# The first forty microseconds of an encoder block: norm weights by transposition, a new load order, and the engines' order written by hand

## The chip, the cores and the metric

The kernel runs on one core of a Trainium2 chip. The metric is the device time of one execution in microseconds (us); a run's figure is the time of the core from launch to end, and a profiled execution also has a span, from its first to its last recorded instruction. Lower is better.

The engines are called by the short names of the profile: PE (TensorE, matmuls; PEld is its weight load), DVE (VectorE), ACT (ScalarE), POOL (GpSimd) and SP (SyncE, which here issues all the DMA transfers).

## The reference

One block of an encoder on a sequence of 1024 tokens with 16 learned meta tokens in front, width 1024, in float32:

```
h = concat(meta, x)                                   # 1040 x 1024
n = rms_norm(h, norm_mix)
proj = n @ w_in            # qa ka va (512 each) | qb 512 | kb 128 | vb 128 | gates ga, gb (1024 each)
y_a = differential attention of 4 heads over all tokens (two softmaxes, difference, rms_norm)
y_b = windowed attention: 8 query heads, 2 key/value heads, window 128, sinks, meta keys
h = h + (sigmoid(ga) * (y_a @ w_ba) + sigmoid(gb) * (y_b @ w_bb)) @ w_o
h = h + (silu(rms_norm(h, norm_ffn) @ w_gate) * (rms_norm(h, norm_ffn) @ w_up)) @ w_down
out = rms_norm(h, norm_final)[16:]
```

`rms_norm(x, g)` is `x * rsqrt(mean(x*x) + 1e-6) * g`.

## The kernel before

**Precision.** Every float32 operand of a matmul is split into a high part (`fp32r`, written by ACT with Copy) and a low part (the difference, written by DVE or POOL); helper `split`, L116 to L118. A product is three matmuls: high x high, high x low, low x high.

**The beginning.** The normed tokens are needed transposed, in `hT_hi` and `hT_lo` (width on the 128 partitions, tokens along the row). Tokens come in tiles of 128: tiles 0 to 7, and `NT`, the 16 meta tokens. For each tile there are three steps:

- `load_x(t)`: SP issues the load of 512 KB into a buffer with the tag `btr`, of which there are four. Tile 4 takes the buffer of tile 0, and so on.
- `norm_x(t)` calls `normed` (L131 to L141): a Square with a running sum on ACT (L134), two small operations on POOL for the reciprocal root (`rstd_of`, L122 and L123), and on DVE one pass that multiplies by it and by the norm weights `gmix` (L140). `gmix` is a tile of 128 x 1024: the 1024 weights, the same in each partition. The kernel before loads it with one DMA that reads the row 128 times.
- `turn_x(t)` calls `transposed` (L143 to L151): twice four transpositions on PE against an identity (L148), the high parts by ACT (L150), the low parts by DVE (L151).

**The first projections.** Three blocks of 128 columns of `w_in` are projected while the tiles come in: kb (`C_KB`), and two blocks of qb, here q0 (`C_QB`) and q1 (`C_QB + P`). `prep` loads a block's weights (1024 rows of 512 bytes, tag `w`, two buffers) and splits them (POOL writes the low part of kb's, DVE that of the q blocks). `project_steps` is a generator: for each chunk of tokens (256 each, kb's last 272) it gives eight steps of three matmuls (L214), and after the eighth an eviction: high part by ACT into one of three stage buffers (tag `qk`), low part by DVE, and then copies by DMA from the stage to `kb` (eight for each chunk, L282, and for the last eight more, L285) or to `qb` (four, L305). `advance(n)` takes the next n steps of the generators in the list `early`, each entry giving one chunk; `ensure(n)` prepares weights ahead. Chunk i needs the tiles 2i and 2i+1. The projection of vb follows, and then the attention in blocks (`attend_b`), whose scores are evicted at L333 with the distance table `tbx` and the sinks `nsink`; these are computed from `iota` (L469 to L477) and small loads (L484 to L499). On POOL, sums of halves of `hT` (`token_sums`, L525 to L539) are wanted for the gates; they need all eight tiles.

**Who sets the order.** The kernel is written in Tile. Where nothing else is said, a planner that simulates the program with its own costs orders each engine's instructions, so that an instruction that stands late in the code may run early. Within `tc.manual_schedule()` the engines (or those named) keep the order of the code. Before, such sections exist only for later parts (POOL from the second half of the windowed attention, PE from the differential attention on, all engines in the last product); the beginning is the planner's.

**Filler matmuls.** Products of zeros into a PSUM bank `idle` that nobody reads keep PE running ahead of the first real work: 15 before the first transpositions and 7 after (L413, L426).

**Activation tables.** ACT loads a table of functions before it uses a function that the current one lacks. There are three such loads: at the start, ahead of the first Sigmoid of the gates (L1010), and ahead of the first Silu (L1304).

Of the kernel before, what the change touches and what calls it, by code (L numbers as in the profile page):

```python
# [19 lines left out]
P = 128  # L20
S = 1024
D = 1024
NM = 16
L = S + NM
DC = D // P
# [48 lines left out]
def encoder_block(ctx: ExitStack, tc: tile.TileContext, x, meta, norm_mix, w_in, lq1, lk1, lq2, lk2,  # L74
# [7 lines left out]
    def f32(ap):  # L82
        return ap.bitcast(F32)
# [76 lines left out]
    def pp_bank(name):  # L160
        return bank(psum1, "pp", name, 3 if psum1 is not psum2 else PP2)
# [45 lines left out]
    def project_steps(col, chunks, name, evac):  # L207
        wh, wl = prepped.pop(col)
        terms = [(wh, hT_hi), (wh, hT_lo), (wl, hT_hi)]
        for at, n in chunks:  # L210
            ps = pp_bank(f"pp_{name}_{at}")
            for c in range(DC):
                for i, (a, b) in enumerate(terms):
                    nc.tensor.matmul(ps[:, :n], a[:, c, :], b[:, c, at:at + n],  # L214
                                     start=(c == 0 and i == 0), stop=(c == DC - 1 and i == 2))
                if c == DC - 1:
                    evac(ps[:, :n], at, n)
                yield
# [51 lines left out]
    vb = [(bpool if g else vtpool).tile([P, 9, P], F32R, tag=("q1", "vb")[g], name=f"vb{g}", bufs=1) for g in range(BG)]  # L270
    mds = [bpool.tile([P, 4, P], F32, name=f"bmd{i}") for i in range(2)]
    for i in range(2):
        nc.gpsimd.memset(f32(vb[i])[:, 8, :], 0.0)
        nc.gpsimd.memset(mds[i], 0.0)

    def kb_consume(st, at, n):
# [103 lines left out]
    def load_x(t):  # L380
        xts[t] = bpool.tile([P, D], F32, tag="btr", name=f"x_{t}", bufs=4)
        if t < NT:
            nc.sync.dma_start(xts[t], x[t * P:(t + 1) * P, :])
        else:
            nc.sync.dma_start(xts[t][:NM], meta)
# [24 lines left out]
    nc.vector.memset(zeros, 0.0)  # L410
    idle = bank(psum1, "by", "idle", 1)
    for _ in range(15):
        nc.tensor.matmul(idle, zeros[:, 0:P], zeros, start=True, stop=True)  # L413
    load_x(0)
    nc.sync.dma_start(gmix, norm_mix.broadcast_to([P, D]))
    load_x(1)
    ensure(1)
    norm_x(0)
    load_x(2)
    norm_x(1)  # L420
    xn0 = xns[0]
    turn_x(0)
    zeros = bpool.tile([P, 512], BF16, tag="by1", name="zeros", bufs=2)
    nc.vector.tensor_scalar(zeros, xn0[:, 0:512], 0.0, None, ALU.mult)
    for _ in range(7):
        nc.tensor.matmul(idle, zeros[:, 0:P], zeros, start=True, stop=True)  # L426
    ensure(2)
    load_x(3)
    norm_x(2)
    turn_x(1)  # L430
    p_kb = project_steps(C_KB, KB_CHUNKS, "kb", evac_split(None, kb_consume))
    p_q0 = qb_steps(0, qb, 0)
    p_q1 = qb_steps(0, qb, 1)
    prepped[C_QB + P] = prep(C_QB + P, "qbx", lowpool, nc.vector)
    early += [(p_kb, DC), (p_q0, DC), (p_q1, DC)]
    advance(E_STEPS)
    norm_x(3)
    turn_x(2)
    advance(E_STEPS)
    load_x(4)  # L440
    norm_x(4)
    turn_x(3)
    early += [(p_kb, DC), (p_q0, DC), (p_q1, DC)]
    advance(E_STEPS)
    load_x(5)
    norm_x(5)
    turn_x(4)
    advance(E_STEPS)
    load_x(6)
    load_x(NT)  # L450
    norm_x(6)
    turn_x(5)
    early += [(p_kb, DC), (p_q0, DC), (p_q1, DC)]
    advance(E_STEPS)
    load_x(7)
    norm_x(7)
    norm_x(NT)
    turn_x(6)
    advance(E_STEPS)
# [24 lines left out]
    nc.sync.dma_start(gsub, subln.rearrange("o p -> p o"), allow_slow_non_contiguous=True)  # L484
    nc.vector.tensor_scalar(gsub, gsub, 1.0 - LAMBDA_INIT, None, ALU.mult)
    sinkb = acon.tile([P, BH], F32, name="sinkb")
    nc.sync.dma_start(sinkb, sink.broadcast_to([P, BH]))
# [3 lines left out]
    lam_in = bpool.tile([P, 4, HD], F32, tag="by1", name="lam_in", bufs=2)  # L491
# [3 lines left out]
    nc.vector.tensor_tensor(lam_p, lam_in[:, 0::2, :], lam_in[:, 1::2, :], ALU.mult)  # L495
# [1016 lines left out]
```

## Time and profile before

| | us |
|---|---|
| median of 3 runs | 1451.38 |
| lowest and highest | 1447.25, 1451.52 |
| the profiled execution's own time | 1446.1 |
| its span | 1444.3 |

Busy time in the profile counts what an engine executes; for PE the ends of matmuls are modelled, since they are pipelined. The timeline lists an instruction's start, its duration, engine, line, operation and tiles (written <- read), and in brackets how long the engine was idle before it and who ended that. "SPq" rows are DMA issues in SP's queue. The chain of waits follows the work that ended last back through what released each step. Views of waits give total, number and longest.

### The profile page before, as it was taken

How to read it: one execution, taken by the hardware profiler on the slowest of the kernel's cores; microseconds unless marked ns; L12 is line 12 of the kernel's file. 1: busy time of each engine (PE TensorE's matmuls, PEld its weight loads, DVE VectorE, ACT ScalarE, POOL GpSimd, SP SyncE). 2: the span in 40 equal slices, each digit the busy share in tenths (PEclk: the TensorE clock that was granted, in tenths of full speed). 3: DMA queues.
4: the chain of work that ended last, by engine and by line, in shares of the span. 5: the costliest groups of instructions: out<-in, count | busy, mean ns of one | idle time of the engine just before them, and what ended most of it. 6: DMA issues, size and time to landing. Idle time of an engine off the chain costs nothing.

```text
span 1444.3 us, 21160 instructions
## 1 busy us (share of the span) xinstructions
PE 1422.8 (99%) x7279; PEld 1221.2 (85%) x7279; DVE 899.2 (62%) x1624; ACT 679.6 (47%) x1290; POOL 641.3 (44%) x605
## 2 busy tenths in 40 slices
PE   8999999999999999999999999999999999999997
PEld 6988989988898999888888878888888888888886
DVE  7478536637697989624614966554555553787567
ACT  6366535545665656544413643333333333444454
POOL 5599127743333333334522665544544452000444
PEclk9999999999999999999999999999999999999999
DMA  8467658986557473576612534333332332964443
GB/s 244 90 209 237 193 162 265 288 281 213 190 169 257 147 227 125 190 256 209 216 34 88 152 104 161 109 102 110 102 102 96 110 102 102 331 208 140 124 129 139
DMA packets 188891, 242.41 MB, mean 168 GB/s; under 512 B 18208, under 2 KB 115936, under 8 KB 188784
## 3 DMA queue, kind: packets, MB, share of 16 engines
q1 hardware_dynamic: 188784, 241.07, 52.6%
q8 instruction: 57, 0.93, 0.3%
q14 instruction: 50, 0.41, 0.1%
HBM read 157.45 MB, written 77.00 MB: 162 GB/s over the span
## 4 chain that ended last, share of the span: by engine, by line
PE 81%; POOL 6%; DVE 5%; issue 4%; DMA 2%; ACT 1%; POOLq 0%; SPq 0%; DVEq 0%; ACTq 0%
PE pg L1293 28%; PE pd L1387 9%; PE pg L737 7%; PE po L1070 6%; PE ppa L780 6%; PE aps L796 3%; PE pp_qb L214 3%; POOL oa L118 3%; PE apy L835 3%; PE pp_ka L214 2%; PE pp_va L214 2%; PE apt L822 2%; PE pp_qa L214 2%; PE bpt L356 1%; PE bpy L362 1%
## 5 line engine op out<-in xcount | busy, mean ns | idle before, releaser
L118 POOL TENSOR_TENSOR wop<-wf,wop 128x512 fp32r<-128x512 f32 x128 | 172.6, 1353 | 165.5 <-ACT wop L117 149.6
L1293 PE MATMUL pg<-t,wop 128*128 128x512 f32 x1056 | 242.6, 389 | 0.0
L1293 PEld LDWEIGHTS pg<-t,wop 128*128 128x128 f32 x1056 | 198.3, 188 | 41.1
L1387 PE MATMUL pd<-ob,oa 128*128 128x512 f32 x924 | 209.9, 389 | 0.4 <-POOL oa L118 0.4
L1387 PEld LDWEIGHTS pd<-ob,oa 128*128 128x128 f32 x924 | 173.4, 188 | 36.8 <-POOL oa L118 0.8
L1293 PE MATMUL pg<-b,wop 128*128 128x512 f32 x792 | 185.6, 392 | 2.3 <-DVE c L1302 2.3
L1293 PEld LDWEIGHTS pg<-b,wop 128*128 128x128 f32 x792 | 149.5, 189 | 34.1 <-issue 2.4
L737 PE MATMUL pg<-hT_hi,gop 128*128 128x512 f32 x384 | 142.7, 396 | 0.0
L118 POOL TENSOR_TENSOR oa<-ra,oa 128x512 fp32r<-128x512 f32 x33 | 44.0, 1335 | 170.1 <-ACT oa L117 168.6
L117 ACT ACTIVATE wop<-wf 128x512 fp32r<-128x512 f32 x128 | 80.2, 631 | 82.9 <-PE pg L1293 48.6
L118 POOL TENSOR_TENSOR gop<-gr,gop 128x512 fp32r<-128x512 f32 x48 | 63.3, 1319 | 116.4 <-ACT gop L117 102.6
L117 ACT ACTIVATE oa<-ra 128x512 fp32r<-128x512 f32 x77 | 48.7, 632 | 105.9 <-PE pd L1387 45.1
L804 ACT ACTIVATE as<-as,amn 128x1040 f32<-128x1040 f32 x64 | 74.5, 1164 | 46.9 <-DVE amn L799 42.8
L1128 DVE TENSOR_TENSOR s<-wf,wf 128x512 f32<-128x512 f32 x22 | 25.0, 1138 | 108.1 <-DMA wf<-in_w_ff_gate_dram 58.0
L796 PE MATMUL aps<-ak,aq 128*128 128x392 f32 (+1 forms) x384 | 90.0, 330 | 1.3 <-DVE amn L799 0.6
L1070 PE MATMUL po<-woh,mT 128*128 128x512 f32 x384 | 88.0, 390 | 0.0
L1070 PEld LDWEIGHTS po<-woh,mT 128*128 128x128 f32 x384 | 71.9, 188 | 14.8
L796 PEld LDWEIGHTS aps<-ak,aq 128*128 128x128 f32 x384 | 69.6, 189 | 15.0 <-DVE amn L799 2.2
L737 PEld LDWEIGHTS pg<-hT_hi,gop 128*128 128x128 f32 x384 | 72.7, 189 | 11.2 <-DVE gk L742 0.2
L343 POOL TENSOR_SCALAR bs<-bs,bdn 128x432 f32<-128x432 f32 (+1 forms) x64 | 41.4, 666 | 85.5 <-DVE bdn L341 73.4
L737 PE MATMUL pg<-hT_lo,gop 128*128 128x512 f32 x192 | 76.0, 396 | 0.0
L807 POOL TENSOR_SCALAR as<-as,adn,neglam 128x1040 f32<-128x1040 f32 x32 | 38.8, 1214 | 62.5 <-DVE adn L805 43.9
(287 smaller groups left out, 3099.0 us busy)
## 6 DMA issues: line engine op xcount, KB each, us to landing
ra<-aop SPq DMA_DIRECT2D x77, 256.0 KB, 2.6
wf<-in_w_ff_gate_dram SPq DMA_DIRECT2D x24, 512.0 KB, 4.0
wf<-in_w_ff_up_dram SPq DMA_DIRECT2D x24, 512.0 KB, 3.9
aop<-as SPq DMA_DIRECT2D x44, 256.0 KB, 2.1
w_c<-in_w_in_dram SPq DMA_DIRECT2D x17, 512.0 KB, 5.7
aop<-c SPq DMA_DIRECT2D x33, 256.0 KB, 2.0
ts_d<-to SPq DMA_DIRECT2D x16, 512.0 KB, 3.7
gw<-in_w_in_dram SPq DMA_DIRECT2D x32, 256.0 KB, 3.9
```

The lines of the kernel that those rows point to most:

```text
L117: nc.scalar.activation(hi, src, AF.Copy)
L118: lo_eng.tensor_tensor(lo, src, f32(hi), ALU.subtract)
L214: nc.tensor.matmul(ps[:, :n], a[:, c, :], b[:, c, at:at + n], start=(c == 0 and i == 0), stop=(c == DC - 1 and i == 2))
L343: nc.gpsimd.tensor_scalar(st[:, r, :W], st[:, r, :W], dn[:, r:r + 1], 1.0, ALU.mult, ALU.mult)
L737: nc.tensor.matmul(ps, op[:, a, c], quad(b, *act)[:, c], start=(p in (2, 5, 1) and c == 0 and i == 0), stop=(p in (2, 3, 4) and c == 3 and ...
L780: nc.tensor.matmul(ps, w[:, a, j, :], src(j, b, tk), start=(j == 0 and n == 0), stop=(j == 3 and n == 2))
L796: nc.tensor.matmul(ps[:, :n], qs[m][:, t * P:(t + 1) * P], ks[m][:, vv, k0:k0 + n], start=(vv == 0), stop=(vv == 1))
L804: nc.scalar.activation(s[m][:, 0:L], s[m][:, 0:L], AF.Exp, bias=low, scale=-1.0, accum_out=dn[:, m:m + 1])
L835: nc.tensor.matmul(py[:, cols], v[:kp, a, k, :], at_[:kp, k, b, :], start=(k == 0 and j == 0), stop=(k == 8))
L1070: nc.tensor.matmul(ps, mT[:, c, a, t * P:(t + 1) * P], wos[q, c][:, b], start=(c == 0 and n == 0), stop=(c == DC - 1 and n == 2))
L1293: nc.tensor.matmul(ps, op[:, x, c, :], b[:, y, c, :], start=(p in (1, 2, 5) and c == 0 and n == 0), stop=(p in (4, 2, 3) and c == 3 and n ...
L1387: nc.tensor.matmul(ps[u], oa[:, a, u * P:(u + 1) * P], ob[:, b, :], start=(p in (1, 2, 5) and j == 0 and k == 0), stop=(p in (2, 3, 4) and ...
```

## The change

- The norm weights are loaded as 8 rows of 128 (`g8`, 4 KB), transposed to `gt8` (128 x 8), and each of the eight columns, broadcast along the row, is transposed once more, which yields the 128 weights in every partition; DVE copies the results to `gmix`.
- SP's order at the start is g8, x0, x1, the weights of kb and q0, x2, the weights of q1, x3. The weights of q1 get a buffer of their own (tag `vb`), and `prep` no longer issues the loads of these three blocks.
- From the zeros to the sixth tile all engines keep the order of the code. In it, chunks follow the tiles they need (chunk 0 of kb, q0 and q1 around tiles 1 to 3; chunk 1 around tiles 4 and 5). The fillers are 6, 10, 4 and 4.
- For the first two chunks of kb, the 24 matmuls are sorted: all eight high x high first, then high x low, then low x high.
- `vb[1]` and the zeroing of two of its blocks come after the projections. The small loads of `gsub`, `sinkb` and the lambdas go into one tile `few`, with a copy for `sinkb`.
- After the last gated product, ACT computes a Silu of one column whose result nobody reads.

```diff
+    asked = {}
+    def ask(col, raw=None):
+        w = asked[col] = (raw or wpool).tile([P, DC, P], F32, tag="vb" if raw else "w", name=f"w_{col}", bufs=1 if raw else 2)
+        nc.sync.dma_start(w, w_in[:, col:col + P].rearrange("(c p) n -> p c n", p=P))
...
     def prep(col, name, p=None, lo_eng=None):
-        w = wpool.tile([P, DC, P], F32, tag="w", name=f"w_{name}", bufs=2)
+        w = asked.pop(col) if col in asked else wpool.tile([P, DC, P], F32, tag="w", name=f"w_{name}", bufs=2)
...
-        else:
+        elif col not in early_cols:
             nc.sync.dma_start(w, w_in[:, col:col + P].rearrange("(c p) n -> p c n", p=P))
...
+    early_cols = (C_KB, C_QB, C_QB + P)
...
+            dots = [(c, i) for c in range(DC) for i in range(3)]
+            if name == "kb" and at < 512:
+                dots.sort(key=lambda d: d[1])
             for c in range(DC):
-                for i, (a, b) in enumerate(terms):
...
+                for d, i in dots[3 * c:3 * c + 3]:
...
+    order_0 = tc.manual_schedule()
+    order_0.__enter__()
     zeros = bpool.tile([P, 512], BF16, tag="by1", name="zeros", bufs=2)
     nc.vector.memset(zeros, 0.0)
     idle = bank(psum1, "by", "idle", 1)
-    for _ in range(15):
-        nc.tensor.matmul(idle, zeros[:, 0:P], zeros, start=True, stop=True)
+    def warm(n):
+        for _ in range(n):
+            nc.tensor.matmul(idle, zeros[:, 0:P], zeros, start=True, stop=True)
+    g8 = bpool.tile([8, P], F32, tag="by1", name="g8", bufs=2)
+    nc.sync.dma_start(g8, norm_mix.rearrange("o (k d) -> (o k) d", k=8))
     load_x(0)
-    nc.sync.dma_start(gmix, norm_mix.broadcast_to([P, D]))
     load_x(1)
+    ask(C_KB)
+    ask(C_QB)
+    load_x(2)
+    ask(C_QB + P, bpool)
+    load_x(3)
+    warm(6)
+    gt8 = small.tile([P, 8], F32, name="gt8", bufs=1)
+    pt8 = pp_bank("pt_g8")[:, 0:8]
+    nc.tensor.transpose(pt8, g8, ident[:8, :8])
+    nc.vector.tensor_copy(gt8, pt8)
+    for b in range(2):
+        pf = pp_bank(f"pf_g{b}")
+        for c in range(4):
+            k = 4 * b + c
+            nc.tensor.transpose(pf[:, c * P:(c + 1) * P], gt8[:, k:k + 1].broadcast_to([P, P]), ident)
+        nc.vector.tensor_copy(gmix[:, 512 * b:512 * b + 512], pf)
+    warm(10)
+    norm_x(0)
+    load_x(4)
+    norm_x(1)
+    load_x(5)
+    turn_x(0)
+    warm(4)
     ensure(1)
...
+    turn_x(1)
+    warm(4)
+    p_kb = project_steps(C_KB, KB_CHUNKS, "kb", evac_split(None, kb_consume))
     ensure(2)
+    p_q0 = qb_steps(0, qb, 0)
+    early += [(p_kb, DC), (p_q0, DC)]
     norm_x(2)
+    advance(DC)
+    prepped[C_QB + P] = prep(C_QB + P, "qbx", lowpool, nc.vector)
     p_q1 = qb_steps(0, qb, 1)
+    advance(DC)
+    turn_x(2)
+    norm_x(3)
+    early += [(p_q1, DC)]
+    advance(6)
+    turn_x(3)
+    advance(2)
+    norm_x(4)
+    load_x(6)
     early += [(p_kb, DC), (p_q0, DC), (p_q1, DC)]
+    advance(DC)
     norm_x(5)
+    load_x(7)
     turn_x(4)
+    advance(DC)
     norm_x(6)
     turn_x(5)
+    advance(DC)
+    order_0.__exit__(None, None, None)
+    load_x(NT)
     norm_x(7)
...
     advance(100)
+    vb.append(bpool.tile([P, 9, P], F32R, tag="vb", name="vb1", bufs=1))
+    for i in range(2):
+        nc.gpsimd.memset(f32(vb[i])[:, 8, :], 0.0)
...
+    few = bpool.tile([P, 5, HD], F32, tag="btr", name="few", bufs=4)
...
+    silu = small.tile([P, 1], F32, tag="silu", name="silu", bufs=1)
+    nc.scalar.activation(silu, gt[:, 0:1], AF.Silu)
```

More of the change, by code (lines that the diff above doesn't have):

```diff
@@ L211, in project_steps @@
             ps = pp_bank(f"pp_{name}_{at}")
+            dots = [(c, i) for c in range(DC) for i in range(3)]
+            if name == "kb" and at < 512:
+                dots.sort(key=lambda d: d[1])
             for c in range(DC):
-                for i, (a, b) in enumerate(terms):
-                    nc.tensor.matmul(ps[:, :n], a[:, c, :], b[:, c, at:at + n],
-                                     start=(c == 0 and i == 0), stop=(c == DC - 1 and i == 2))
+                for d, i in dots[3 * c:3 * c + 3]:
+                    a, b = terms[i]
+                    nc.tensor.matmul(ps[:, :n], a[:, d, :], b[:, d, at:at + n],
+                                     start=((d, i) == dots[0]), stop=((d, i) == dots[-1]))
                 if c == DC - 1:
@@ L269, in encoder_block @@
     kb = [(bpool if g else lowpool).tile([P, 2, NT, 144], F32R, tag=("k1", "kb")[g], name=f"kb{g}", bufs=1) for g in range(BG)]
-    vb = [(bpool if g else vtpool).tile([P, 9, P], F32R, tag=("q1", "vb")[g], name=f"vb{g}", bufs=1) for g in range(BG)]
+    vb = [vtpool.tile([P, 9, P], F32R, tag="q1", name="vb0", bufs=1)]
     mds = [bpool.tile([P, 4, P], F32, name=f"bmd{i}") for i in range(2)]
     for i in range(2):
-        nc.gpsimd.memset(f32(vb[i])[:, 8, :], 0.0)
         nc.gpsimd.memset(mds[i], 0.0)
@@ L418, in encoder_block @@
[L418 to L426, printed above, removed]
+    ask(C_KB)
[6 more added lines that the diff above has]
+    pt8 = pp_bank("pt_g8")[:, 0:8]
@@ L435, in encoder_block @@
-    early += [(p_kb, DC), (p_q0, DC), (p_q1, DC)]
[L436 to L445, printed above, removed]
+    advance(DC)
[7 more added lines that the diff above has]
+    load_x(6)
+    early += [(p_kb, DC), (p_q0, DC), (p_q1, DC)]
+    advance(DC)
     norm_x(5)
+    load_x(7)
@@ L447, in encoder_block @@
     turn_x(4)
-    advance(E_STEPS)
-    load_x(6)
-    load_x(NT)
+    advance(DC)
     norm_x(6)
     turn_x(5)
-    early += [(p_kb, DC), (p_q0, DC), (p_q1, DC)]
-    advance(E_STEPS)
-    load_x(7)
+    advance(DC)
+    order_0.__exit__(None, None, None)
+    load_x(NT)
     norm_x(7)
@@ L458, in encoder_block @@
     turn_x(6)
+    early += [(p_kb, DC), (p_q0, DC), (p_q1, DC)]
     advance(E_STEPS)
@@ L482, in encoder_block @@
     nc.gpsimd.memset(far_a, 3e38)
+    few = bpool.tile([P, 5, HD], F32, tag="btr", name="few", bufs=4)
     gsub = acon.tile([P, 1], F32, name="gsub")
-    nc.sync.dma_start(gsub, subln.rearrange("o p -> p o"), allow_slow_non_contiguous=True)
-    nc.vector.tensor_scalar(gsub, gsub, 1.0 - LAMBDA_INIT, None, ALU.mult)
+    nc.sync.dma_start(few[:, 4, 0:1], subln.rearrange("o p -> p o"), allow_slow_non_contiguous=True)
+    nc.vector.tensor_scalar(gsub, few[:, 4, 0:1], 1.0 - LAMBDA_INIT, None, ALU.mult)
     sinkb = acon.tile([P, BH], F32, name="sinkb")
-    nc.sync.dma_start(sinkb, sink.broadcast_to([P, BH]))
+    nc.sync.dma_start(few[:, 4, 8:8 + BH], sink.broadcast_to([P, BH]))
+    nc.vector.tensor_copy(sinkb, few[:, 4, 8:8 + BH])
     nsink = acon.tile([P, BH], F32, name="nsink")
@@ L490, in encoder_block @@
     neglam = acon.tile([P, 1], F32, name="neglam")
-    lam_in = bpool.tile([P, 4, HD], F32, tag="by1", name="lam_in", bufs=2)
+    lam_in = few
     for i, v in enumerate((lq1, lk1, lq2, lk2)):
@@ L494, in encoder_block @@
     lam_p = bpool.tile([P, 2, HD], F32, tag="bys", name="lam_p", bufs=1)
-    nc.vector.tensor_tensor(lam_p, lam_in[:, 0::2, :], lam_in[:, 1::2, :], ALU.mult)
+    nc.vector.tensor_tensor(lam_p, lam_in[:, 0:4:2, :], lam_in[:, 1:4:2, :], ALU.mult)
     lam_s = acon.tile([P, 2], F32, name="lam_s")
```

5 lines of the change are left out of this document (removed).

## The prediction

> **What bounds the kernel now.** I read the page first, for the shares and the chain of waits.
>
> ```profile
> span 1444.3 us, 21160 instructions
> PE 1422.8 (99%) x7279; PEld 1221.2 (85%) x7279; DVE 899.2 (62%) x1624; ACT 679.6 (47%) x1290; POOL 641.3 (44%) x605
> PE 81%; POOL 6%; DVE 5%; issue 4%; DMA 2%; ACT 1%; POOLq 0%; SPq 0%; DVEq 0%; ACTq 0%
> ```
>
> TensorE is the bound, so an edit helps where TensorE has nothing to do, and its busy share hides such places because matmul ends are modelled. For the start I therefore went to the chain in order of time, whose pieces give the pace of matmuls that follow each other closely.
>
> ```profile
> 31.31 0.87 PE ptn_a L148 x8
> ...
> 41.95 5.61 PE pp_qb L214 x48
> 47.56 3.02 PE pp_kb L214 x24
> ...
> 56.23 7.35 PE pp_vb L214 x42
> ```
>
> A 256-column matmul costs 5.61/48 = 0.117 us, so a chunk of 24 costs 2.81 us, and the eight transpositions of a token tile cost 0.87 us. The start consists of 12 chunks (kb, q0, q1, four each; one is the 3.02 us chunk) and nine tiles, the last small (I put it at 0.7 us): 11 x 2.81 + 3.02 + 8 x 0.87 + 0.7 = 41.6 us of TensorE work. It begins with the first tile's transpositions and ends where vb's projection begins. The timeline of TensorE shows the beginning:
>
> ```profile
> 1.17 4.86 PE L413 MATMUL idle<-zeros 128*128 128x512 bf16 x15 [1.17 <-DVE zeros L410]
> 7.89 1.09 PE L148 MATMUL ptn_a<-ident,xn_a 128*128 128x128 f32 x8 [1.86 <-DVE xn_a L140]
> 11.43 1.10 PE L148 MATMUL ptn_a<-ident,xn_a 128*128 128x128 f32 x8 [0.93 <-DVE xn_a L140]
> 24.15 0.50 PE L214 MATMUL pp_qb<-hT_hi,wb_qbx 128*128 128x256 f32 x2 [1.53 <-DVE wb_qbx L118]
> ```
>
> From 7.89 to 56.23 is 48.3 us, so the start loses 48.3 - 41.6 = 6.7 us after its first transposition. That is nearly all a new order can win; the 7.89 us ahead of it wait for the first tile of x. One limit more: 0.3% of the time is 4.4 us, about what a measurement of this kernel can tell from no change.
>
> **The loads.** The timeline of the load queue and of ScalarE, which waits for the landings, and one row of the DMA view (issue to landing last):
>
> ```profile
> 0.72 0.39 SPq L383 DMA_DIRECT2D x<-in_x_dram  x1
> 1.16 0.42 SPq L415 DMA_DIRECT2D gmix<-in_norm_mix_dram  x1
> 4.43 1.06 ACT L134 ACTIVATE xn_a<-x 128x1024 f32<-128x1024 f32 x1 [2.43 <-DMA x<-in_x_dram]
> 7.83 1.06 ACT L134 ACTIVATE xn_a<-x 128x1024 f32<-128x1024 f32 x1 [2.25 <-DMA x<-in_x_dram]
> gmix<-in_norm_mix_dram SPq DMA_DIRECT2D x1, 512.0 KB, 5.3
> ```
>
> Before, 512 KB of broadcast weights stand between x0 and x1. After, g8 (4 KB) stands ahead of x0, so x0 is issued one slot (0.44 us) later and lands at about 4.87. x1 moves to gmix's old place in the bytes: 1.16 + 5.3 + 0.44 = 6.9, not 7.83. So tile 0 is 0.44 us later and tile 1 is 0.9 us earlier. The three projection weights now come before x3, and x2 follows two of them. The rows give 7.83 - 4.43 = 3.4 us for two loads of 512 KB, 1.7 each, so kb's weights land at 8.6, then q0's at 10.3, x2 at 12.0, q1's at 13.7 and x3 at 15.4. ScalarE, as worked out below, reaches them at 10.0, 12.1, 13.15, 15.3 and 19.5: each is covered by 1.2 to 4 us, and what comes later than that counts in full.
>
> Durations that recur, from the timelines of the engines:
>
> ```profile
> 6.55 1.28 DVE L140 SCALAR_TENSOR_TENSOR xn_a<-x,rstd_a,gmix 128x1024 f32<-128x1024 f32 x1 [5.44 <-POOL rstd_a L123]
> 17.54 1.09 ACT L150 ACTIVATE hT_hi<-ptn_a 128x512 fp32r<-128x512 f32 x2 [0.93 <-PE ptn_a L148]
> 12.76 0.69 DVE L151 TENSOR_TENSOR hT_lo<-ptn_a,hT_hi 128x512 fp32r<-128x512 f32 x1 [0.78 <-ACT hT_hi L150]
> 12.64 1.06 ACT L117 ACTIVATE wh_c<-w_c 128x1024 fp32r<-128x1024 f32 x1
> 10.97 2.64 POOL L118 TENSOR_TENSOR wl_c<-w_c,wh_c 128x1024 fp32r<-128x1024 f32 x1 [1.07 <-ACT wh_c L117]
> 19.55 0.38 ACT L232 ACTIVATE qk_stage<-pp_kb 128x256 fp32r<-128x256 f32 x1
> ```
>
> g8's landing is a price the trace lacks. Its nearest rows are small copies:
>
> ```profile
> qb<-qk_stage SPq DMA_DIRECT2D x32, 64.0 KB, 2.0
> sinkb<-in_sink_logits_dram SPq DMA_DIRECT2D x1, 4.0 KB, 5.9
> ```
>
> The second queued behind megabytes; g8 has nothing ahead of it, so I take 2.0, landing at 2.7, with 5.9 as the far end. Then come six warming matmuls (to 3.1 at the pace of the first row of TensorE's timeline), one transposition, a small copy, eight transpositions and two 128x512 copies by VectorE (0.69 us each by the row of the low parts), gmix being ready between 5.5 and 6. It is wanted when tile 0's rstd is ready, at 4.87 + 6.55 - 4.43 = 7.0. The far end would have it ready near 9 and cost 2 us. The Trainium skill ("DMA: Bandwidth & Descriptors", Anatomy of one DMA) gives about 2.0 us fixed per transfer for another kind of queue; by it the result would be that of the near end.
>
> **The hand order, step by step.** From the start of a tile's Square to the end of its norm takes 6.55 + 1.28 - 4.43 = 3.4 us when nothing is in the way, and two hi parts are done about 1.7 us after the transpositions begin (half of 0.87, then 1.09, and the hand-overs). I assume that every engine runs the traced order of the code.
>
> - Tile 0: transposed from 8.33. ScalarE: its hi parts to 10.0, the kb weights' high part to 11.06, tile 1's hi parts to 12.1 (tile 1's norm ended at 10.3, its transpositions at 11.2), the q0 weights to 13.15, then the Square of tile 2 to 14.3.
> - TensorE: kb chunk 0 from 12.1, high terms first, so that the low parts (VectorE, 12.9) and the low weights (GpSimd, 11.1 + 2.64 = 13.7) hide behind the terms before. Both end inside 2.81 us: done at 14.95. q0 chunk 0 to 17.75. Tile 2 to 18.6.
> - ScalarE then does tile 2's hi parts to 19.5 before the Square of tile 3, because the code has that order: tile 3's norm ends at 19.5 + 3.4 = 22.9. TensorE has six steps of q1 (18 x 0.117 = 2.1) to do, till 20.7, and waits 2.2 us.
> - Tile 3, the last two q1 steps (24.5), a short wait for hi parts (24.65), kb chunk 1 to 27.45. The Square of tile 4 stands behind q1's eviction (25.1): norm ends at 28.5, a wait of 1.0 us.
> - Tile 4 to 29.4, q0 chunk 1 to 32.2, tile 5 to 33.05, q1 chunk 1 to 35.85. Tile 6's Square follows q0's eviction (32.8), so its norm ends at 36.2: 0.3 us lost.
> - The rest, ordered by the planner: three tiles (2.4) and six chunks (17.1), ending at 36.2 + 19.5 = 55.7.
>
> Against 56.23 that is **0.6 us earlier**. The reorder removes the 1.53 us wait for q1's weights; two waits for norms take its place.
>
> **What is moved past queues.** SP: x6 and x7 now stand behind the copies of staged chunks, and so do the small loads for sinks and lambdas.
>
> ```profile
> 20.70 6.31 SPq L282 DMA_DIRECT2D kb<-qk_stage  x8
> kb<-qk_stage SPq DMA_DIRECT2D x16, 64.0 KB, 3.1
> 55.15 0.48 DVE L236 SCALAR_TENSOR_TENSOR qk_stage<-pp_qb,qbs,qk_stage 128x256 fp32r<-128x256 f32 x1 [2.78 <-ACT qk_stage L235]
> 65.05 0.52 DVE L333 CUSTOM_DVE_ANT_0 bs<-bps,tbx,nsink 128x288 f32<-128x288 f32 x1 [6.90 <-PE bps L331]
> ```
>
> Eight copies occupy SP for 6.3 us. x7 follows kb chunk 1's copies (chunk done at 27.45, its low part evicted near 28.9), which end at 35.2, so it lands near 38 and its norm ends near 41.4; chunks 3 want it at about 45. Covered, by 4 us. A fourth eviction needs the first stage buffer back: kb chunk 0's copies end at 16.8 + 6.3 + 3.1 = 26.2, the eviction comes at 27.5. Covered, by 1.3 us, and behind it in ScalarE's queue would wait the Square of tile 5. The distance tables leave VectorE's first 43 us and fit into its later idle time (2.78 and 6.90 us in two of the rows).
>
> GpSimd: its token sums wait for tile 7, which comes about 8 us later.
>
> ```profile
> 35.47 1.64 POOL L525 TENSOR_TENSOR ta<-hT_hi 128x512 f32<-128x512 f32 x1 [3.83 <-ACT hT_hi L150]
> 73.32 1.96 POOL L343 TENSOR_SCALAR bs<-bs,bdn 128x288 f32<-128x288 f32 x4 [14.77 <-DVE bdn L341]
> ```
>
> Its idle 14.77 us ahead of 73.32 takes those 8 up; I price it at nothing.
>
> **The Silu table.** Four rows of the timeline, of ScalarE and TensorE:
>
> ```profile
> 734.03 0.63 ACT L117 ACTIVATE woh<-wo 128x512 fp32r<-128x512 f32 x1 [16.12 <-PE po L1070]
> 818.63 1.28 ACT L1304 ACT_TABLE_LOAD   x1
> 819.93 0.64 ACT L1304 ACTIVATE c<-c 128x512 f32<-128x512 f32 x1
> 833.56 6.63 PE L1293 MATMUL pg<-b,wop 128*128 128x512 f32 x21 [1.99 <-DVE c L1302]
> ```
>
> The load moves into 16 us of idle ScalarE at 718 and costs nothing there. Its 1.28 us at 818 lie beside matmuls; what they could have delayed is the 1.99 us wait at 833. VectorE ends that wait, and it is hardly idle from 817 on, so the gain lies between 0 and 1.28; I take 0.3. Silu follows the load after 1.30 us. The Trainium skill ("ScalarE: Activation LUTs", What ACT_TABLE_LOAD costs) puts a switch at about 2.66 us, a drain included; by it the gain could reach the whole 1.99. The trace does not show that drain between load and Silu, so the row decides.
>
> **Sum.** -0.6 - 0.3, about -0.9 us. The profiled execution took 1446.1 us (span 1444.3 and 1.8 around it), so its like would take 1445.2. The three runs lie at 1447.25, 1451.38 and 1451.52, the profiled one below all of them; as their level I take the middle of the range, 1449.4, and forecast 1448.5.
>
> **The rivals.**
>
> 1. Faster: the waits for norms do not come. If ScalarE gets to the Squares of tiles 3 and 4 before TensorE runs out, 2.2 + 1.0 + 0.3 us go too, TensorE being dense from 12.1 on; with the whole 1.28 us at the Silu and the 1.0 us of the row below, since the copies on SP would end earlier, this is -0.6 - 3.5 - 1.28 - 1.0 = -6.4, some 1443.
>
> ```profile
> PE bps L331 <- DVE bmn L333: 1.0, 3, 0.5
> ```
>
> For it: one early Square is all it takes. Against it: tile 3's Square stands behind tile 2's hi parts in the code. Chance 0.29.
>
> 2. Slower: GpSimd becomes the bound after 70 us. The token sums start some 8 us later; the planner, not the hand order, places them. If it puts them among the attention blocks and leaves GpSimd's 14.77 us idle as they are, 8 us of sums join an engine that carries the chain there (6% of all), and TensorE, short of projections, waits for most of it: +6, some 1455. It decides from the point where over half of the 8 us stays outside the idle stretch. For it: the chain goes through GpSimd from 73 on. Against: the idle stretch is long enough. Chance 0.14.
>
> 3. The hand order does not move the end: with loads at full rate tile 1 lands no earlier, everything shifts by 0.44 us and the weights' wait returns elsewhere: +0.5 to +2, some 1450.5. Chance 0.10.
>
> **How the numbers follow.** My forecast has 0.47. A gain over 4.4 us needs rival 1 nearly whole, or a lucky plan beyond it (0.29, to which the forecast's edge adds 0.03: 0.32); a loss over 4.4 us needs rival 2 or g8's far end on top of rival 3 (0.14 and 0.03: 0.17); the rest, 0.51, is no change. The forecast's own range is 1445 to 1452: the level's spread of 4.3 us and -2 to +1 for the terms. With rivals 1 and 2 it is 1441 to 1455.5.
>
> **What would show it.** In the changed profile: first Square near 4.9, second near 6.9; no 512 KB load of gmix; kb's matmuls from 12.1 in runs of eight; a wait of TensorE near 21 and one near 28, both ended by VectorE's norm; vb's projection beginning near 55.7; a table load near 718 and none near 818; the wait near 833 hardly shorter. I am wrong if the waits near 21 and 28 are missing, if vb begins before 53 or after 59, or if the time moves although vb begins where I say: then the planner's part or GpSimd did it.

## The result: 0.9% slower, and the profile after

| | before | after |
|---|---|---|
| median, 4 runs each on one chip (us) | 1451.21 | 1462.89 |
| lowest and highest | 1447.25, 1451.52 | 1462.19, 1464.55 |
| ratio after to before, 95% interval | | 1.0088, 1.0069 to 1.0108 |
| span of the profiled execution | 1444.3 | 1460.4 |
| vb's projection begins, in the profiled execution | 56.1 | 66.5 |

I had forecast 1448.5 with 1441 to 1455.5 around it. The change costs some 12 us. The page of after, its span, PE's share and the chain:

```profile
span 1460.4 us, 21190 instructions
PE 1428.6 (98%) x7290; PEld 1222.9 (84%) x7290; DVE 906.9 (62%) x1627; ACT 679.7 (47%) x1291; POOL 640.3 (44%) x605
PE 81%; POOL 4%; issue 4%; DMA 4%; DVE 4%; ACT 1%; SPq 1%; POOLq 0%; DVEq 0%; ACTq 0%
```

PE is the bound as before; nothing here says where 12 us went. The timeline of PE does (start, duration, then in brackets the idle time ahead and who ended it):

```profile
8.42 1.10 PE L148 MATMUL ptn_a<-ident,xn_a 128*128 128x128 f32 x8 [0.47 <-DVE xn_a L140]
...
12.04 1.29 PE L225 MATMUL pp_kb<-hT_hi,wh_c 128*128 128x256 f32 x8
...
23.04 1.06 PE L148 MATMUL ptn_a<-ident,xn_a 128*128 128x128 f32 x8 [2.01 <-DVE xn_a L140]
...
28.80 1.06 PE L148 MATMUL ptn_a<-ident,xn_a 128*128 128x128 f32 x8 [1.17 <-DVE xn_a L140]
...
55.16 1.00 PE L148 MATMUL ptn_a<-ident,xn_a 16*128 16x16 f32 x8 [8.16 <-DVE xn_a L140]
```

The part ordered by hand came out as forecast: tile 0 at 8.42 (8.33), kb at 12.04 (12.1), waits of 2.01 and 1.17 us (2.2 and 1.0). Then, in the part that the planner still orders, PE stands still for 8.16 us until the meta tile is normed. What DVE and POOL did meanwhile:

```profile
44.15 0.65 DVE L505 CAST dist<-it 128x960 f32<-128x960 int32 x1
...
48.12 4.70 DVE L505 CAST dist<-it 128x960 f32<-128x960 int32 x1
52.74 2.27 DVE L140 SCALAR_TENSOR_TENSOR xn_a<-x,rstd_a,gmix 16x1024 f32<-16x1024 f32 x1
```

```profile
46.30 1.11 POOL L123 TENSOR_TENSOR rstd_a<-rstd_a,neg_half 16x1 f32<-16x1 f32 x1
47.38 1.25 POOL L562 TENSOR_TENSOR ta<-hT_hi 128x512 f32<-128x512 f32 x1
...
51.05 1.25 POOL L564 TENSOR_TENSOR ta<-ta,tal 128x512 f32<-128x512 f32 x1
```

The same work in before, from the timelines of DVE, PE and SP, and last the meta tile's load in after:

```profile
26.80 0.65 DVE L470 CAST dist<-it 128x960 f32<-128x960 int32 x1
...
32.72 0.65 DVE L470 CAST dist<-it 128x960 f32<-128x960 int32 x1
```

```profile
38.90 0.42 PE L148 MATMUL ptn_a<-ident,xn_a 16*128 16x16 f32 x4
```

```profile
18.54 0.35 SPq L385 DMA_DIRECT2D x<-in_meta_tokens_dram  x1
```

```profile
40.60 0.58 SPq L395 DMA_DIRECT2D x<-in_meta_tokens_dram  x1
```

The meta tile's factor was ready at 47.4. Ahead of its norm in DVE's queue stood a copy of the distance tables. Such a copy took 0.65 us where it began with POOL idle (44.15, and both times in before), and it took 4.70 while POOL ran four token sums back to back: it ended at 52.82, just after the fourth sum (52.3). The Trainium skill ("SBUF — State Buffer", Who interferes with whom) says that a copy by DVE in a two-port mode and a POOL instruction exclude one another for their whole length, the first to issue having the port; by these rows the trace agrees, though none names the mode, and the copy lost to four in a row. The meta tile itself was late: its load was issued at 40.60, behind the copies of staged chunks, against 18.54 before.

PE paid a second time, by its clock. The windows of after (length, PE's busy time with the matmuls counted in parentheses, then the granted clock):

```profile
44.00:48.00 4.00, 2.99 (x26) 1.00 0.35 84
48.00:52.00 4.00, 0.00 (x0) 0.68 0.41 100
52.00:56.00 4.00, 0.84 (x8) 0.50 0.07 16
56.00:60.00 4.00, 4.00 (x21) 0.54 0.24 53
60.00:64.00 4.00, 4.00 (x34) 1.00 0.24 66
```

21 matmuls instead of 34 in the first whole window after the wait: 13 x 0.117, some 1.5 us more.

The Silu table is loaded at 731 beside a busy PE, none at 830, and the wait that I had hoped to shorten is as long as before (1.88 against 1.99):

```profile
731.09 1.28 ACT L1084 ACT_TABLE_LOAD   x1
846.88 7.34 PE L1332 MATMUL pg<-b,wop 128*128 128x512 f32 x24 [1.88 <-DVE c L1341]
```

And there is a loss where nothing seemed to be changed. In the feed-forward part PE streams operands called b (`b11`, `b21`, `b22`: transposed normed tokens) and t (their sums and differences) against the weights `wop`, without gaps, at clock 1.00. Two rows of before, then the same two of after:

```profile
1036.55 11.04 PE L1293 MATMUL pg<-b,wop 128*128 128x512 f32 x48
1009.35 16.48 PE L1293 MATMUL pg<-t,wop 128*128 128x512 f32 x72
```

```profile
1012.77 11.17 PE L1332 MATMUL pg<-b,wop 128*128 128x512 f32 x48
1023.78 16.53 PE L1332 MATMUL pg<-t,wop 128*128 128x512 f32 x72
```

Over 792 b matmuls and 1056 t matmuls that is 792 x 0.13/48 + 1056 x 0.05/72 = 2.9 us. The stretch from the first to the last t matmul took 386.0 us in two profiles of before and 388.7 in after. So: 10.4 us at the start and 2.7 to 2.9 in the feed-forward part. They need not add up exactly to the difference of the medians, because the attention between them varies from one execution to the next (the gated products that follow it began at 622.3 in one profile of before, at 629.1 in the other).

### The profile page after: what moved, and what is told of

Its sections match the earlier page's. It is cut to its first block, busy times and chain, and to the rows that moved or that the text cites. A ratio compares the mean times of both kernels' runs of the same rounds, so it can differ in the third digit from the quotient of the medians.

```text
span 1460.4 us, 21190 instructions
## 1 busy us (share of the span) xinstructions
PE 1428.6 (98%) x7290; PEld 1222.9 (84%) x7290; DVE 906.9 (62%) x1627; ACT 679.7 (47%) x1291; POOL 640.3 (44%) x605
## 4 chain that ended last, share of the span: by engine, by line
PE 81%; POOL 4%; issue 4%; DMA 4%; DVE 4%; ACT 1%; SPq 1%; POOLq 0%; DVEq 0%; ACTq 0%
PE pg L1332 28%; PE pd L1426 9%; PE pg L774 7%; PE po L1109 6%; PE ppa L817 6%; PE pp_va L225 3%; PE pp_qa L225 3%; PE aps L833 3%; PE apy L872 3%; POOL oa L118 3%; PE pp_ka L225 2%; PE apt L859 2%; PE pp_qb L225 2%; PE bpt L366 2%; PE bps L341 2%
## 5 line engine op out<-in xcount | busy, mean ns | idle before, releaser
L117 ACT ACTIVATE oa<-ra 128x512 fp32r<-128x512 f32 x77 | 48.7, 632 | 106.8 <-PE pd L1426 47.4
L841 ACT ACTIVATE as<-as,amn 128x1040 f32<-128x1040 f32 x64 | 74.6, 1165 | 48.2 <-DVE amn L836 44.1
L1167 DVE TENSOR_TENSOR s<-wf,wf 128x512 f32<-128x512 f32 x22 | 23.8, 1080 | 107.0 <-DMA wf<-in_w_ff_gate_dram 57.5
```

The source lines that it names most:

```text
L117: nc.scalar.activation(hi, src, AF.Copy)
L841: nc.scalar.activation(s[m][:, 0:L], s[m][:, 0:L], AF.Exp, bias=low, scale=-1.0, accum_out=dn[:, m:m + 1])
```

## The experiments

The first four expectations were written while I took the one wait at the meta tile for the loss at the start; letters in them mean what they say there. From the fifth on, theory A is wider: the hand order is sound, but it holds every engine, so that the small work which the planner used to place early (meta tile, distance tables, small loads) falls behind it, among token sums and the last evictions. Its rivals are that the other edits cost the time (B), or the late token sums (D). Where an expectation speaks of "the fillers inside the hand order", it means these three groups of small work, not the filler matmuls. Ratios are to runs of before on the same chip, with 95% intervals.

**Before against itself.**

> The kernel before, unchanged, profiled a second time. The profiled execution of before was 5 us under the median of its runs, so the profiles differ by 16.1 us of span where the medians differ by 11.7. If the difference beyond the start (2 us in the differential attention, 2.7 us in the feed-forward part) belongs to the change, this profile shows the feed-forward products p=1..7 in 386 us as the first one did. If it belongs to the execution, this profile takes 388 to 390 us there. Time: ratio 1.000.

1448.89 us, ratio 1.0004 (0.9989 to 1.0019). A few us, as in after, can be told from nothing. The feed-forward stretch took 386.0 us again, so the longer one in after belongs to the change.

**The meta tile inside the hand order.**

```diff
     load_x(6)
+    load_x(NT)
...
     turn_x(5)
+    norm_x(NT)
     advance(DC)
+    turn_x(NT)
     order_0.__exit__(None, None, None)
-    load_x(NT)
```

> The changed kernel with the meta tile's load, norm and transpositions inside the hand order (load after x6, norm after tile 5's transpositions, transpositions after q1's chunk 1). Theory A (TensorE stands 8.2 us at the meta tile's transpositions, because VectorE's second int-to-float copy of the distance table, blocked for 4.7 us beside GpSimd's token sums, is ahead of the meta tile's norm; then it runs 4 us at half clock): wait gone, vb's projection begins near 57 instead of 66.5, gain 8.5 to 10.5 us, ratio to before 1.000 to 1.002. Rival B (the late token sums make GpSimd the bound, the stall is only where it shows): gain under 2 us, ratio 1.007 or more.

1459.86 us, ratio 1.0078 (1.0048 to 1.0107): the 8.16 us wait is gone, but theory A's gain of 8.5 to 10.5 us did not come. The number is rival B's. The timelines of PE, DVE and POOL show why:

```profile
60.78 0.44 PE L225 MATMUL pp_vb<-hT_hi,wh_c 128*128 128x384 f32 x1 [2.40 <-DVE qk_stage L244]
...
63.27 0.53 PE L225 MATMUL pp_vb<-hT_hi,wh_c 128*128 128x384 f32 x1 [1.86 <-DVE qk_stage L247]
```

```profile
56.08 0.15 DVE L521 TENSOR_SCALAR gsub<-few 128x1 f32<-128x1 f32 x1 [5.72 <-DMA few<-in_subln_gain_dram]
...
57.11 2.06 DVE L524 COPY sinkb<-few 128x8 f32<-128x8 f32 x1 [0.21 <-DMA few<-in_sink_logits_dram]
...
60.30 0.43 DVE L244 TENSOR_TENSOR qk_stage<-pp_kb,qk_stage 128x272 fp32r<-128x272 f32 x1
60.65 2.16 DVE L532 TENSOR_TENSOR lam_p<-few 128x128 f32<-128x128 f32 x1
62.74 0.47 DVE L247 SCALAR_TENSOR_TENSOR qk_stage<-pp_qb,qbs,qk_stage 128x256 fp32r<-128x256 f32 x1
```

```profile
56.31 2.83 POOL L118 TENSOR_TENSOR wl_c<-w_c,wh_c 128x1024 fp32r<-128x1024 f32 x1
```

PE is now done with the chunks near 58.4 and meets the next jam. DVE waits 5.72 us for a small load (issued behind staged copies, into `few`, which shares its buffers with the token tiles), then needs 2.06 us for a copy of eight columns beside POOL's 2.83 us split (the copy ended at 59.17, the split at 59.14); the evictions of the last chunks stand behind these in its queue, and PE waits for their PSUM banks. vb begins 5.7 us earlier than in after, but behind the second wait PE runs at a granted clock of 0.50 (windows 64 to 66), and vb's last matmul starts at 76.9, only 2.9 us earlier than in after (79.8; before 67.9). So the meta tile was only the first of the waits.

**The tables' copy moved to ACT.** `nc.vector.tensor_copy(dist[:, cols], it)` becomes `nc.scalar.copy(...)`.

> The changed kernel with only the two int-to-float copies of the distance table moved from VectorE to ScalarE. Theory A: the meta tile's norm no longer stands behind the blocked copy; its rstd was ready at 47.4, so its transpositions come near 49 to 50.5 instead of 55.2, TensorE waits 2 to 3.5 us and its clock stays full: gain 5 to 8 us, ratio to before 1.002 to 1.005. Rival B: gain under 2 us.

1462.23 us, ratio 1.0091 (1.0061 to 1.0120). The copies take 0.98 us each on ACT, PE has no wait at the meta tile (transposed at 47.14), although the meta tile's load is still issued at 40.79. So the late load alone did not make the wait in after; the blocked copy did. Theory A's gain of 5 to 8 us did not come, since PE stops at the same next place:

```profile
60.93 0.69 PE L225 MATMUL pp_vb<-hT_hi,wh_c 128*128 128x384 f32 x1 [4.12 <-DVE qk_stage L244]
```

**Filler matmuls in the gap.** 34 products of zeros ahead of the meta tile's transpositions.

> The changed kernel with 34 filler matmuls (about 7.3 us) between the last matmul of chunk 2 and the meta tile's transpositions; nothing else is freed. Theory A with the clock as its second part: the wait stays, but the granted clock stays at 1.0 from 48 to 60 us and the 256-column matmuls after it cost 0.117 us instead of 0.21: gain 1.5 to 2.5 us, ratio 1.007. If the clock costs nothing: no gain, ratio 1.009.

1469.66 us, ratio 1.0144 (1.0111 to 1.0177). The clock held 1.00 from 48 to 64, but the planner now ordered DVE otherwise: the meta tile's low part came at 64.35, behind the tables and the first small loads (in after at 56.58), PE waited 3.76 us for it, and vb began at 73.6. The copy on DVE took 4.71 us again, and again ended just after POOL's fourth sum. What the clock alone costs stays at the 1.5 us read above; this run doesn't show it.

```profile
PE pp_kb L225 <- DVE hT_lo L151: 3.8, 1, 3.8
```

**No hand order, all other edits kept.** The two lines of `order_0` and its exit taken out.

> The changed kernel without the hand order: the planner orders the whole beginning again; the transposed norm weights, the early loads, the small loads through one tile, the later second value tile and the early Silu stay. Theory A (the hand order holds every engine, so that the distance tables, the small loads and the meta tile run behind it, among GpSimd's token sums and the last evictions): the tables run between 20 and 45 again, vb's projection begins at 55.5 to 58.5, ratio to before 0.998 to 1.003 (1448 to 1455). Theory B (the cost is in the other edits: the small loads' buffer, shared with the token tiles, and the early Silu): the small loads still come behind the last copies, vb begins after 60, ratio 1.005 to 1.009.

1460.14 us, ratio 1.0071 (1.0055 to 1.0088). The ratio, vb at 60.5 and the late small loads are theory B's numbers, although the tables run at 28 to 42 again, as A says. So taking the hand order out does not bring the time back. The planner makes little of the other edits, and the first tiles come late, because DVE copies the turned norm weights into `gmix` only at 13.06, behind a low part of weights (11.44):

```profile
15.78 3.36 PE L148 MATMUL ptn_a<-ident,xn_a 128*128 128x128 f32 x16 [6.08 <-DVE xn_a L140]
```

The small loads are issued only at 76. The last score products of the windowed attention, whose evictions need the sinks, start 8.3 us later than in one profile of before and 5.6 later than in the other. The late small loads, then, do not need the hand order. I put them down to the edit to `few`, whose buffers are shared, without a run that shows this alone. The late first tiles are something that the hand order repairs.

**All three groups inside the hand order.** Meta tile as above; the tables counted straight into `dist`, the absolute value in one instruction, so that they share no buffer; the small loads in a buffer that the zeros leave free.

```diff
     ensure(2)
+    few = small_loads()        # six loads, tag "by1"
+    count(0)                   # iota into dist itself
...
     turn_x(2)
+    count(1)
+    cast(0)
     norm_x(3)
+    cast(1)
...
     advance(2)
+    absolute(0)                # max(-1 * dist, dist)
     norm_x(4)
     load_x(6)
+    load_x(NT)
...
     turn_x(5)
+    norm_x(NT)
     advance(DC)
+    absolute(1)
+    window()                   # tbx
+    turn_x(NT)
+    small_work(few)
     order_0.__exit__(None, None, None)
```

> The changed kernel with three groups of work put inside the hand order: the meta tile (load, norm, transpositions), the distance tables (counted straight into their own buffer, the absolute value in one instruction, no buffer shared with the token tiles) and the small loads with their arithmetic. Theory A: nothing is left behind the hand order but token tiles, chunks and token sums; vb's projection begins at 55.5 to 57.5 and ends by 69, no wait of TensorE over 1.5 us between 46 and 66; time 1448 to 1453, ratio 0.998 to 1.002. Theory B: the time stays at 1457 to 1463, ratio over 1.004. Theory D (GpSimd's token sums alone, which now run 12 us later, hold the evictions back): the waits near 56 to 62 stay, vb ends after 72.

1451.87 us, ratio 1.0018 (1.0007 to 1.0028): 10 of the 12 us are back, as theory A had it. The rows of DVE and PE that answer to those above:

```profile
20.33 0.65 DVE L435 CAST dist<-dist 128x960 f32<-128x960 int32 x1
...
46.40 0.16 DVE L456 COPY sinkb<-few 128x8 f32<-128x8 f32 x1
...
46.67 0.28 DVE L458 TENSOR_TENSOR few<-few 128x128 f32<-128x128 f32 x1
```

```profile
58.17 0.34 PE L225 MATMUL pp_vb<-hT_hi,wh_c 128*128 128x384 f32 x1
```

The same copies and products take 0.65, 0.16 and 0.28 us instead of 4.70, 2.06 and 2.16; vb begins at 58.2 without a wait, 0.7 us behind theory A's latest. Theory D falls with it: the token sums begin at 48.83, as late as in after (47.38; before 35.47), and PE does not wait for them.

**The Squares of tiles 3 and 4 ahead**, as rival 1 of the prediction had it: `norm_x(3)` before `turn_x(2)`, `norm_x(4)` before the six steps.

> As the kernel with the fillers inside the hand order, and the norms of tiles 3 and 4 put ahead of tile 2's and tile 3's transpositions, as rival 1 of the prediction had it. Theory A: the waits near 23 (2.0) and 28.8 (1.2) go, vb begins 2.5 to 3.2 us earlier than there, at 52.5 to 55; time 1445 to 1450, ratio 0.996 to 1.000. If the end does not follow the start: vb begins earlier but the time is within 1 us of the kernel without this edit.

1452.32 us, ratio 1.0018 (1.0009 to 1.0027): nothing, and vb begins at 59.3, later than without this edit, so neither theory's start came. In the view of waits the norms' waits shrink from 3.9 us to 1.2, and waits for low parts (1.1 before this edit) take their place:

```profile
PE pp_kb L225 <- DVE hT_lo L151: 3.2, 2, 1.8
PE ptn_a L148 <- DVE xn_a L140: 1.2, 2, 1.0
```

**One group left behind.** First the small loads (in the change's own code), then the tables, with the rest as in the kernel with all three inside.

> The kernel with the fillers inside the hand order, but the small loads and their arithmetic left where the change has them: behind the distance tables' place, in a buffer shared with the token tiles. Theory A, small loads' part (VectorE's queue holds the last evictions behind arithmetic that waits for loads issued after 50): a wait of TensorE of 2 to 6 us between 54 and 64, ended by an eviction, and half clock behind it; vb begins at 60 to 63 and ends after 74; 4 to 8 us more than with them inside, 1456 to 1460. If the tables and the meta tile were the whole loss: within 1 us of 1451.9.

1455.03 us, ratio 1.0034 (1.0021 to 1.0046). The forecast wait did not come: vb begins at 57.5. But this kernel does not put the small loads where the change has them. With the tables out of the shared buffers, the first two are issued at 39.97, and their copy runs ahead of the token sums:

```profile
44.82 0.17 DVE L559 COPY sinkb<-few 128x8 f32<-128x8 f32 x1
```

> The kernel with the fillers inside the hand order, but the distance tables left behind it, in the change's own code and buffers; meta tile and small loads inside. If the tables carry the loss (their copies run beside GpSimd's token sums, as the 4.70 us copy did): VectorE's table instructions take 2 us and more, a wait of TensorE of 3 to 8 us between 46 and 62, vb ends after 74, 1456 to 1461. If the loss needs tables and small loads together: 1452 to 1455, no such wait.

1453.8 us, ratio 1.0039 (1.0020 to 1.0059), vb at 59.0, no such wait. The tables, too, ran ahead of the token sums, as they did in the kernel with only the meta tile inside (37.65 and 40.37):

```profile
37.88 0.65 DVE L549 CAST dist<-it 128x960 f32<-128x960 int32 x1
...
40.60 0.64 DVE L549 CAST dist<-it 128x960 f32<-128x960 int32 x1
```

So neither kernel sets the group that it leaves behind beside a busy POOL, and whether one group alone would make the jam is not shown. The second shows something else. It differs from the kernel with only the meta tile inside in nothing but the small loads, their place and their buffer, and in it vb's last matmul starts at 71.5 instead of 76.9, with 1.0039 instead of 1.0078. By the medians the late small loads are the greater part of that jam, some 5 to 6 us; the two ratios were taken on different chips.

What a single group left behind costs here, 2 to 3 us, is less certain: both intervals overlap that of the kernel with all three inside, and no wait of PE over 1.2 us follows 50. With the small loads left behind, PE waits twice for DVE in the windowed attention, 1.9 us together, which it does not do with all three inside; whether that is the loss is not shown.

**The early Silu alone**, in before.

> The kernel before with the early Silu alone. If the early Silu costs or gains nothing: the stretch of the feed-forward steps (first to last gate matmul of the later groups) is 386.0 as in before, ratio 0.999 to 1.001. If it is what lengthened that stretch in all changed kernels: 388.7 to 389.2, ratio 1.0015 to 1.0025. If my forecast for it was right: 0.3 us less, ratio 0.9998, not to be told from one.

1453.91 us, ratio 1.0030 (1.0019 to 1.0041), stretch 391.5. An instruction on an idle engine costs 4 us? But for it and its table load, the order on every engine is that of before. What differs are addresses: `silu` is a new tile of 32 bytes in the pool of small tiles, and every buffer of that side of the memory moves on by 32 bytes in each partition, b among them, while t and `wop` stay. In after `gt8` and `silu` make it 64. The next kernels tell address from table.

**A new small tile and no Silu**, and **the Silu without a new tile**:

```diff
+    idle_tile = small.tile([P, 1], F32, tag="silu", name="silu", bufs=1)
+    nc.gpsimd.memset(idle_tile, 0.0)
```

```diff
+    silu = small.tile([P, 1], F32, tag="rstd", name="silu")
+    nc.scalar.activation(silu, gt[:, 0:1], AF.Silu)
```

> The kernel before with one more small tile of 32 bytes a partition, which GpSimd sets to zero where the early Silu stood; the Silu table is loaded where it was before. Theory P: b's matmuls take 0.230 us, the stretch is 391 to 392, ratio 1.0025 to 1.004, as with the early Silu in its own tile. Theory S: 386.0, ratio 0.999 to 1.001.

> The kernel before with the early Silu, written into a slot of the tiles that hold the norms' factors, so that no address changes. Theory P: stretch 386.0, b's matmuls 0.2225 us, ratio 0.9985 to 1.001 (the table load itself: 0 to 1.3 us gained, my forecast 0.3). Theory S: 388 to 392, ratio 1.002 to 1.004.

1454.01 us, ratio 1.0032 (1.0020 to 1.0044), for the tile; 1448.75 us, ratio 1.0002 (0.9992 to 1.0011), for the table. The stretch is 391.5 and 386.0. The tile is the whole cost, the table is worth nothing that can be measured. One row of b matmuls each, from the timelines of PE:

```profile
1041.74 11.37 PE L1295 MATMUL pg<-b,wop 128*128 128x512 f32 x48
```

```profile
1038.91 11.04 PE L1295 MATMUL pg<-b,wop 128*128 128x512 f32 x48
```

**Moved on to 128 bytes.** The kernel with all three groups inside, and 64 unused bytes more in the small pool.

> The kernel with the fillers inside the hand order, and 64 unused bytes more in the pool of small tiles, so that all buffers behind it lie 128 bytes further than in before, instead of 64. Theory P (a new small tile shifts the operand b of the feed-forward matmuls off a boundary of 128 bytes, and each of its 792 matmuls streams more slowly: 0.2225 us at 0 bytes, 0.2257 at 64, 0.2304 at 32): the b matmuls are back at 0.222 to 0.223 us, the stretch of the later groups at 386.0 instead of 389.2, time 2.5 to 3 us less than without the padding, 1448.5 to 1449.5, ratio 0.999 to 1.000. Theory S (the early Silu, not the address, slows the stretch): 389 and 1451 to 1453 as without the padding.

1452.49 us, ratio 1.0023 (1.0013 to 1.0033): no gain, and b is as slow as with 32 bytes (stretch 390.8). My boundary of 128 fell.

```profile
1042.69 11.36 PE L1352 MATMUL pg<-b,wop 128*128 128x512 f32 x48
```

**Moved by 256**, in before, with unused bytes ahead of b in its own pool; and **b kept, what follows moved** by 32, with the bytes behind it. One execution each.

> The kernel before with 256 unused bytes ahead of the three b operands in their own pool. If what counts is that b and the weights agree modulo 256 bytes: b's matmuls at 0.2225 us, stretch 386.0. If any shift of b costs: 0.2257 to 0.2304, stretch 388.5 to 392.

> The kernel before with 32 unused bytes behind the three b operands: b stays, the buffers behind it (token sums, sums of weights, collected products) move by 32 bytes. If it is b's own address: 0.2225 us, stretch 386.0. If the writers' buffers decide: 0.230 us, stretch 391 to 392.

1451.91 and 1448.52 us; one execution each cannot tell these times apart, but the rows can. In this order:

```profile
1042.29 11.04 PE L1294 MATMUL pg<-b,wop 128*128 128x512 f32 x48
```

```profile
1038.91 11.04 PE L1294 MATMUL pg<-b,wop 128*128 128x512 f32 x48
```

It is b's own address that counts, and 256 bytes are as good as none. In the built program of before, b begins at byte 2688 of each partition, which is 128 modulo 256, like `wop` and t. 48 b matmuls take 11.04 us there, 11.37 at 32 bytes on, 11.17 at 64, 11.36 at 128, and 11.04 at 256. Whether b must agree with `wop`, or have that remainder in itself, is open: `wop` was not moved.

**Both causes removed.** The kernel with all three groups inside, `gt8` and `silu` in slots of the tag `rstd`, so that b stays at 2688.

> The kernel with the fillers inside the hand order, the turned norm weights and the early Silu's result each in a slot of the tiles that hold the norms' factors, so that no buffer of the feed-forward part moves. If the two causes add up: stretch 386.0, b's matmuls 0.2225 us, 2.5 to 3.5 us less than with the new tiles (1451.9), 1448 to 1449.5, ratio 0.999 to 1.001 to before. If the start is really better than before's: below 1446, ratio under 0.998.

1449.85 us, ratio 1.0005 (0.9993 to 1.0017); 48 b matmuls take 11.04 us, and the stretch is 386.5 instead of 389.2. Of after's 0.88%, putting the small work inside gives back 0.7%. Keeping b's address gives back 0.13% here (0.3% in before); that step is within the intervals, and it is the rows and the stretch that show it. What is left of the change is no different from before, and its start is not better: vb begins at 58.8, against 56.1. No version tried beats before.

## Why the prediction was wrong, point by point

- **The hand order, step by step: right.** Tile 0, the second Square (6.30 for 6.9), kb chunk 0, the waits for the norms of tiles 3 and 4 came within 0.6 us of their times. That this order beats the planner's start was not seen, though: with the small work inside as well, vb began at 58.2, not at 55.7, and PE took 49.8 us from its first transposition to vb, against 48.2 in before.
- **"The rest, ordered by the planner: three tiles (2.4) and six chunks (17.1)": the step that failed.** I priced the planner's part as if PE ran on without gaps. It took 8.16 us of waiting and some 1.5 us of half clock more, and vb began at 66.5, not 55.7. The wait was for the meta tile's norm, behind a table copy that POOL's token sums blocked.
- **"The distance tables leave VectorE's first 43 us and fit into its later idle time": wrong by the way I costed it.** DVE's idle time there is real, but an in-order queue is not a bag of idle time: what is moved into it stands ahead of norms and evictions. And I gave the tables no duration at all: each copy took 0.65 us in before, with POOL idle, and one took 4.70 in its new place, with POOL busy.
- **The token sums "at nothing": half right.** They came 11.9 us later (47.38 for 35.47), not 8, and did not hold POOL back later: from the first to the last score product the windowed attention took 224.8 us, against 224.3 and 226.7 in the two profiles of before, so rival 2's mechanism is not seen. But they made DVE's copies long.
- **The small loads** were named among what moves behind the staged copies, and not priced at all. They set the second jam: with them inside as well, 1.0078 became 1.0039.
- **The meta tile's load** moved behind the copies too (18.54 to 40.60); I priced x7 there and left the meta tile out.
- **The Silu: right that it is worth about nothing** (0.3 forecast; 1.0002 measured without a new tile). That the new small tiles (`gt8` and `silu`) move the address of a streamed operand was in no term of the sum: 2.7 to 2.9 us.
- **Rival 1** was tried: the Squares ahead remove 2.7 us of waits for norms and gain nothing.
- The range missed because every unpriced item that the runs found lay on the slow side; my own sign for error ("if vb begins after 59") was the right one.

## What to carry to other kernels

An order by hand that holds all engines pushes whatever it does not list behind it; list the small work too. Taking the hand order out was no cure here, since the small loads stayed late and the first tiles became so (1.0071). Before an instruction is priced at its old duration in a new place, look at what the other engines run there, here DVE's copies beside POOL. And removing the first wait is worth what the next one leaves: here the meta tile's 8.16 us gave 0.1% until the queue behind it was cleared too. After adding a tile, compare the pace of gapless matmul runs far away, since a new tile moves addresses.

## What the runs showed of the hardware

- DVE beside a busy POOL: a copy of 128x960 took 4.70 us instead of 0.65, one of 128x8 2.06 instead of 0.16, a product with two inputs in memory (128x128) 2.16 instead of 0.28.
- PE's last matmul ahead of the wait ended at 47.0. The granted clock was still 1.00 in the window from 49.00 to 49.25 and 0.50 from 49.50 on, so it dropped after some 2.5 us without matmuls. PE resumed at 55.16, and the clock was 0.50 until 59.5 and 1.00 in the window from 60. The Trainium skill ("TensorE: Matmul & The Clock Gate", What's actually happening) puts the drop after an idle window of about 3.4 us; the trace does not agree, the drop came sooner, and the measurement decides.
- The address of the streamed operand b set the pace of its 512-column matmuls at full clock: 48 take 11.04 us at a start of 128 modulo 256, and 1% to 3% more (11.17 to 11.37) at the three other remainders seen.
